# Block sums of feed-forward weights made in DRAM by accumulating transfers, and twelve more K pairs in seven products

## The chip, the cores and the metric

The kernel runs on one core of a Trainium2 chip. The metric is the device time of one execution in microseconds (us); lower is better. Weights and activations are float32. TensorE multiplies in the float32r format, and every float32 operand is split into a high and a low part (`hi`, `lo`), so a product of two operands is three matmuls: high x high, high x low, low x high.

## The reference

Two decoder layers on a sequence of 256 tokens with 2048 features. Layer 0 is a Mamba-2 SSD mixer, layer 1 differential attention; each is followed by a gated feed-forward of width 5632, with norms before and after.

```python
def swiglu(h, w_gate, w_up, w_down):
    return (jax.nn.silu(h @ w_gate) * (h @ w_up)) @ w_down

def reference(x, ...):
    for i in range(DEPTH):          # DEPTH = 2
        h = rmsnorm(x, norm_mix_pre[i])
        m = ssd_mixer(h, ...) if i % 2 == 0 else diff_attention(h, ...)
        x = x + rmsnorm(m, norm_mix_post[i])
        h = rmsnorm(x, norm_ffn_pre[i])
        x = x + rmsnorm(swiglu(h, ffn_w_gate[i], ffn_w_up[i], ffn_w_down[i]), norm_ffn_post[i])
    return x
```

## The kernel before

**Stages.** One TensorE stream runs through the SSD mixer (weights `w_zxbc`, then `w_so`), the first feed-forward (`w_g0`, `w_u0`, `w_d0`), attention, and the second feed-forward. The 256 tokens are two tiles `t` of 128. Weights come in blocks of 128 partitions x 4 x 512 floats (1 MB). A block is loaded by SP's queue into a `raw` buffer (three of them; in the feed-forwards two `rawm` buffers join, picked by a counter in `raw_tile`). `prep` makes `hi` by a copy on ScalarE and `lo` by a subtraction on VectorE.

**Pairs of column chunks.** In the feed-forwards `pair` works on two column chunks `c` and `c+1` of 512 columns at once. The contraction runs over K pairs: `kp` is a pair of 128-row K tiles. For one K pair the weights are a 2x2 grid of blocks (two K tiles by two chunks), and the activations another 2x2 grid (two token tiles by two K tiles). Multiplied out, a K pair takes eight products of three matmuls each. For the K pairs in the list `seven`, a Winograd form takes seven products: `p1`, `p5`, `p6`, `p7` and three sums that go straight into the accumulators. It needs sums and differences of the four weight blocks (`sh`, `sl`, split like a weight), and of the activations (`forms`, made by `make_form` into `ff` buffers, of which there are four in the pool's tag `xr`). The weight sums are made as follows: a GpSimd transfer adds block 1 onto block 0 of `raw` in SBUF while it loads (`accum_op=ALU.add`), and VectorE makes the other three in three additions, with four ScalarE copies and two more VectorE subtractions for `sh` and `sl`.

**Which K pairs.** `SEVEN = (2, 4, 6)` and `SEVEN_G = (2, 3, 4, 6)` name them for gate and up. `PARTS` walks the 11 chunks of the feed-forward in three parts, with the chunks of a part, then the K groups of the down projection that are ready behind it, then for chunk pairs 0 and 2 of the down projection the groups taken in seven products. `g_done` and `u_done` close a pair with the activation. The down projection's partial results of the first two parts are kept in the DRAM tiles `md`; those of the second part are added there by GpSimd's transfers (L733).

**The SSD stage.** Weights for z, B, C and x run through `mv` (24 matmuls a block). Beside them runs the scan: for every head group `g` and token tile `c`, `decay_load` fetches `mt` (SP), ScalarE makes the decay of it, and GpSimd multiplies it with `cbm` (L530). TensorE's `py` (L580) reads `mt`; its `pyo` (L612) reads `xdt`, which GpSimd has scaled (L608). GpSimd also takes the reciprocal roots `rs_g` (L97) of the gated norm, without which the transposes `pt_s` (L303) can't run.

**What sets the order.** The program is written with a step counter: `tick()` counts, and `later(k, fn)` puts `fn` k steps further. A list scheduler then places the instructions of each engine and queue, with the written order as priority; the place of an instruction can therefore differ from where the step counter puts it. At run time every engine and queue works through its own list in order, held by semaphores alone. A transfer started from GpSimd stands in GpSimd's list, and one from SyncE in SP's.

Of the kernel before, what the change touches and what calls it, by code (L numbers as in the profile page):

```python
# [16 lines left out]
P = 128  # L17
# [22 lines left out]
PARTS = [((10, 0, 1), (20, 0, 21, 1, 2, 3), {0: (21,), 2: (21, 2)}),  # L40
         ((2, 3, 4, 5), (4, 5, 8, 6, 9, 7, 10, 11), {0: (6, 7), 2: (6, 7)}),
# [4 lines left out]
def trunk_kernel(ctx, tc, x_rows, x_cols, vec_cols, vec64, post_rows, lam_rows,  # L46
# [177 lines left out]
    def pair(blocks, stat, seven, form, done):  # L224
# [20 lines left out]
        for kp, src in enumerate(blocks):  # L245
            raw = raw_tile()
            for c in range(2):
                nc.sync.dma_start(raw[:, 2 * c:2 * c + 2], src[c])
            if kp in seven:

                nc.gpsimd.dma_start(raw[:, 0:1], src[0][:, 1:2], accum_op=ALU.add)
# [12 lines left out]


            sh = hl[0].tile([P, 4, 512], F32R, tag="hi", name=f"sh{seq[0]}")
            sl = hl[0].tile([P, 4, 512], F32R, tag="lo", name=f"sl{seq[0]}")
            nc.vector.tensor_tensor(raw[:, 2], raw[:, 2], raw[:, 0], op=ALU.add)
            nc.scalar.copy(sh[:, 0], raw[:, 0])
            nc.scalar.copy(sh[:, 2], raw[:, 2])  # L270
            nc.vector.tensor_tensor(raw[:, 1], raw[:, 2], raw[:, 1], op=ALU.subtract)
            nc.scalar.copy(sh[:, 1], raw[:, 1])  # L272
            nc.vector.tensor_tensor(raw[:, 3], raw[:, 3], raw[:, 2], op=ALU.add)
            nc.scalar.copy(sh[:, 3], raw[:, 3])
            nc.vector.tensor_tensor(sl[:, 0:3], raw[:, 0:3], sh[:, 0:3].bitcast(F32), op=ALU.subtract)  # L275
            nc.vector.tensor_tensor(sl[:, 3], raw[:, 3], sh[:, 3].bitcast(F32), op=ALU.subtract)
# [5 lines left out]
            mm("p5", form(kp, 0), sh[:, 1], sl[:, 1], last)  # L282
            mm("p7", form(kp, 1), sh[:, 0], sl[:, 0], last)
# [488 lines left out]

    for half in range(2):
        if half == 0:
            later(2, dt_load)
            later(4, lambda: row_stats(0))
            later(5, lambda: (row_stats(1), dt_split()))
            later(7, halve)
            later(8, dt_product)
            later(8, lambda: later(1, make_rstd_bc(rstd_bc, rs0, lambda: s1.tile([P, P], F32, tag="dg", name="dg"))))  # L780
            later(10, dt_chain)
            later(15, dt_token)
            z_chunk(0, x_first_stat, z0_raw)
# [41 lines left out]
    def make_form(dct, key, stat, t512, keep=None):  # L825

        xf = t512("xf", (P, NT, 2, P))
        f = t512("f", (P, 4, P))
        for t in range(NT):
            for j in range(2):  # L830
                hi, lo = stat(key, j, t)
                nc.vector.tensor_tensor(xf[:, t, j], hi.bitcast(F32), lo.bitcast(F32), op=ALU.add)
        nc.vector.tensor_tensor(f[:, 0], xf[:, 1, 0], xf[:, 1, 1], op=ALU.subtract)
        nc.vector.tensor_tensor(f[:, 1], xf[:, 1, 0], xf[:, 0, 0], op=ALU.subtract)
        nc.vector.tensor_tensor(f[:, 2], xf[:, 0, 0], f[:, 0], op=ALU.subtract)
        nc.vector.tensor_tensor(f[:, 3], xf[:, 0, 1], f[:, 2], op=ALU.subtract)
        ff = dct[key] = xr_tile("ff", (P, 4, 2, P), F32R)
        split(ff[:, :, 0], ff[:, :, 1], f)
        if keep:
            nc.sync.dma_start(keep, ff.rearrange("p f h q -> p (f h q)").bitcast(F32))  # L840
# [22 lines left out]
    def ffn(wg, wu, wd, step, final):  # L863
# [17 lines left out]
        def kg_stat(kg, j, t):  # L881
            hi, lo = lookup(acts, (t, kg // 2))
            return hi[:, kg % 2 * 2 + j], lo[:, kg % 2 * 2 + j]

# [32 lines left out]
        for k, kp in enumerate(SEVEN_F):  # L917
            keep[kp] = dramp.tile([P, 8 * P], F32, name=f"form{step}_{kp}")
            later(1 + 3 * k, lambda kp=kp: make_form(forms, kp, kp_stat, t512, keep[kp]))
        mv([wu[10, k] for k in range(4)], u_stat, u_evac, LAG2)  # L920
        def form_later(k, kg):
            later(k, lambda: make_form(dforms, kg, kg_stat, t512))
# [5 lines left out]
        for pi, (part, kgs, two) in enumerate(PARTS):  # L928
# [12 lines left out]
            for c in part:  # L941
                if c < 10 and c % 2 == 0:
                    if c == part[-2]:
                        form_later(6, two[0][0])
                    pair(twos(wg, c), kp_stat, SEVEN_G if pi and c != part[-2] else SEVEN, form, g_done(c // 2))
                    if c == part[-2] and len(two[0]) > 1:
                        form_later(6, two[0][1])
                    pair(twos(wu, c), kp_stat, SEVEN_G if pi and c != part[-2] else SEVEN, form, u_done(c // 2))
            if pi == 0:
                form_later(8, two[2][1])  # L950
# [11 lines left out]
    ffn(w_g0, w_u0, w_d0, 1, False)  # L962
# [187 lines left out]
```

## Time and profile before

| | |
|---|---|
| time, median of 3 runs | 2525.58 us (2525.24 to 2525.67) |
| the profiled execution | 2525.76 us, span 2524.0 us |
| TensorE busy | 2505.5 us (99%), 11834 matmuls |
| VectorE, ScalarE, GpSimd busy | 1943.7 us (77%), 1412.9 us (56%), 233.4 us (9%) |
| SP's transfers (q1) | 503.96 MB, 57.5% of the 16 DMA engines' time |
| GpSimd's transfers (q0) | 35.13 MB, 7.0% |
| granted TensorE clock | 0.999 |

The SSD stage lies from 0 to some 700 us, the first feed-forward ends at 1357 us, the second starts near 1840 us. Matmuls overlap, so the mean length shown for one of them (about 390 ns) is more than what one adds to the time. A transfer's share is the time that its packets took, summed, over 16 engines times the stretch.

### The profile page before, as it was taken

To read this page: it belongs to the slowest core of one execution; us is meant where nothing else is said; L and a number is where in the kernel's file an instruction comes from. 1 tells how busy PE (TensorE), PEld (TensorE's weight loads), DVE (VectorE), ACT (ScalarE), POOL (GpSimd) and SP (SyncE) were. 2 spreads that over 40 slices of the span, in tenths; PEclk is the share of its full clock that TensorE was granted. 3 is DMA by queue.
4 is the path that set the end of the run, shared out by engine and by line. 5 is a ranking of instruction groups with operands and counts; after the bars stand their busy time and mean duration, and the time that the engine had idled before them with its cause. 6 is when DMAs were issued, how large, how long until landed. Compare 5 with 4: busy or idle time off the path is not lost.

```text
span 2524.0 us, 31572 instructions
## 1 busy us (share of the span) xinstructions
PE 2505.5 (99%) x11834; PEld 2066.3 (82%) x11834; DVE 1943.7 (77%) x2410; ACT 1412.9 (56%) x1915; POOL 233.4 (9%) x226
## 2 busy tenths in 40 slices
PE   9999999999999999999999999999999999999998
PEld 8878888888888888888888888887888888888886
DVE  6777547777688899978997765566688889878985
ACT  5767556666565455555554654455555465546553
POOL 0121000110110010001001100001100100010002
PEclk9999999999999999999999999999999999999999
DMA  7555556555786786768676544544776967686774
GB/s 286 194 169 183 193 189 200 169 182 186 254 275 204 251 256 212 253 216 259 214 253 229 192 149 167 184 150 148 249 228 205 295 217 231 220 271 220 229 246 153
DMA packets 143387, 541.44 MB, mean 215 GB/s; under 512 B 14401, under 2 KB 31105, under 8 KB 116225
## 3 DMA queue, kind: packets, MB, share of 16 engines
q1 hardware_dynamic: 125872, 503.96, 57.5%
q0 software_dynamic: 16992, 35.13, 7.0%
q8 instruction: 93, 1.52, 0.2%
q10 hardware_dynamic: 368, 0.32, 0.1%
q14 instruction: 62, 0.50, 0.1%
HBM read 520.41 MB, written 18.94 MB: 214 GB/s over the span
## 4 chain that ended last, share of the span: by engine, by line
PE 94%; DVE 2%; ACT 1%; issue 1%; DMA 1%; POOL 1%; SPq 0%; DVEq 0%; ACTq 0%; POOLq 0%
PE acc L242 38%; PE acc L191 34%; PE cp L242 9%; PE acc L216 5%; PE acc L218 2%; DVE lo L138 1%; PE sc L1026 1%; PE pt_f L303 1%; PE py L580 1%; DMA mt<-acum_d 1%; ACT hi L137 0%; PE ptx L666 0%; PE po L1062 0%; PE pc L487 0%; PE px L567 0%
## 5 line engine op out<-in xcount | busy, mean ns | idle before, releaser
L138 DVE TENSOR_TENSOR lo<-raw,hi 128x2048 fp32r<-128x2048 f32 (+2 forms) x401 | 733.9, 1833 | 302.1 <-ACT hi L137 298.0
L137 ACT CAST hi<-raw 128x2048 fp32r<-128x2048 f32 (+2 forms) x401 | 605.3, 1510 | 449.2 <-PE acc L191 140.3
L191 PE MATMUL acc<-hi,xT 128*128 128x512 f32 x1792 | 583.7, 397 | 0.1
L242 PE MATMUL acc<-hi,xT 128*128 128x512 f32 x1608 | 518.5, 390 | 0.0
L191 PEld LDWEIGHTS acc<-hi,xT 128*128 128x128 f32 x1792 | 335.7, 188 | 71.5 <-issue 3.0
L242 PEld LDWEIGHTS acc<-hi,xT 128*128 128x128 f32 x1608 | 301.8, 188 | 62.6
L191 PE MATMUL acc<-lo,xT 128*128 128x512 f32 x896 | 351.7, 393 | 1.4 <-DVE lo L138 1.4
L242 PE MATMUL acc<-lo,xT 128*128 128x512 f32 x804 | 312.9, 389 | 0.0
L138 DVE TENSOR_TENSOR lo<-rawm,hi 128x2048 fp32r<-128x2048 f32 (+1 forms) x87 | 181.8, 2089 | 35.3 <-ACT hi L137 32.1
L137 ACT CAST hi<-rawm 128x2048 fp32r<-128x2048 f32 (+1 forms) x87 | 152.7, 1756 | 96.6 <-PE acc L242 62.3
L191 PEld LDWEIGHTS acc<-lo,xT 128*128 128x128 f32 x896 | 168.6, 188 | 36.6 <-DVE lo L138 3.8
L216 PE MATMUL acc<-xT,hi 128*128 128x512 f32 x512 | 180.5, 398 | 0.0
L242 PEld LDWEIGHTS acc<-lo,xT 128*128 128x128 f32 x804 | 150.9, 188 | 31.4
L242 PE MATMUL acc<-hi,ah_f 128*128 128x512 f32 x450 | 176.1, 391 | 0.0
L242 PE MATMUL acc<-hi,al_f 128*128 128x512 f32 x450 | 175.2, 389 | 0.0
L242 PE MATMUL acc<-lo,ah_f 128*128 128x512 f32 x450 | 175.2, 389 | 0.0
L242 PE MATMUL cp<-sh,ff 128*128 128x512 f32 x516 | 172.8, 389 | 0.0
L218 PE MATMUL acc<-xT,lo 128*128 128x256 f32 x512 | 143.0, 281 | 0.0
L142 DVE SCALAR_TENSOR_TENSOR lo<-raw,cols,hi 128x512 fp32r<-128x512 f32 x128 | 92.4, 766 | 57.5 <-ACT hi L141 57.2
L141 ACT ACTIVATE hi<-raw,cols 128x512 fp32r<-128x512 f32 x128 | 84.6, 715 | 59.0 <-PE acc L191 41.3
L216 PEld LDWEIGHTS acc<-xT,hi 128*128 128x128 f32 x512 | 96.2, 188 | 23.0
L275 DVE TENSOR_TENSOR sl<-raw,sh 128x1536 fp32r<-128x1536 f32 x54 | 94.9, 1757 | 24.0 <-ACT sh L272 21.5
(298 smaller groups left out, 4101.4 us busy)
## 6 DMA issues: line engine op xcount, KB each, us to landing
raw<-in_w_zxbc_dram SPq DMA_DIRECT2D x77, 1024.0 KB, 4.8
raw<-in_w_d_dram SPq DMA_DIRECT2D x98, 512.0 KB, 5.8
raw<-in_w_g_dram SPq DMA_DIRECT2D x96, 512.0 KB, 6.0
raw<-in_w_u_dram SPq DMA_DIRECT2D x96, 512.0 KB, 5.9
raw<-in_w_qkv_dram SPq DMA_DIRECT2D x48, 1024.0 KB, 4.7
raw<-in_w_so_dram SPq DMA_DIRECT2D x32, 1024.0 KB, 4.7
rawm<-in_w_g_dram SPq DMA_DIRECT2D x64, 512.0 KB, 6.2
rawm<-in_w_u_dram SPq DMA_DIRECT2D x64, 512.0 KB, 5.7
```

The source lines that it names most:

```text
L137: nc.scalar.copy(hi, raw)
L138: nc.vector.tensor_tensor(lo, raw, hi.bitcast(F32), op=ALU.subtract)
L141: nc.scalar.activation(hi[:, j], raw[:, j], AF.Copy, scale=scale[j])
L142: nc.vector.scalar_tensor_tensor(lo[:, j], raw[:, j], scale[j], hi[:, j].bitcast(F32), op0=ALU.mult, op1=ALU.subtract)
L191: nc.tensor.matmul(acc[t], a, b[:, j], start=(i == 0 and j == 0 and q == 0), stop=(i == last and j == 1 and q == 2))
L216: nc.tensor.matmul(acc[ct], hi[:, j, cs], x.rearrange("p a s -> p (a s)"), start=(i == 0 and j == 0), stop=False)
L218: nc.tensor.matmul(acc[ct][:, :S], lo[:, j, cs], x[:, 0], start=False, stop=(i == last and j == 1))
L242: nc.tensor.matmul(acc[k], a, b, start=first and q == 0, stop=last and q == 2)
L275: nc.vector.tensor_tensor(sl[:, 0:3], raw[:, 0:3], sh[:, 0:3].bitcast(F32), op=ALU.subtract)
L303: nc.tensor.transpose(pt[:, j], src[:, j * P:(j + 1) * P], ident)
L580: nc.tensor.matmul(py[e * 64:(e + 1) * 64, a], xd[c][:, 2 * a + e], mts[c][:, 2 * a + e], start=True, stop=True)
L1026: nc.tensor.matmul(sc[c][:, h], qT[cp, h % 2, ts], kT[cp, h % 2, :nk * P], start=True, stop=True)
```

## The change

A new function `sums_of` is called ten times ahead of the SSD stage, for gate and up of chunk pairs 0, 2, 4, 6 and 8 of the first feed-forward. Each call makes a DRAM tile `bs` that holds, for K pairs 2 and 3, the four block sums that the seven products need. It copies three pieces from the weights (SP, DRAM to DRAM) and adds four pieces onto them (GpSimd, `accum_op`), two from the weights and two from the tile itself. `pair` gets a dictionary `ready`; for a K pair in it, it loads three blocks of the weights and the 1 MB of sums, and prepares both with `prep`, in place of the adding transfer and the VectorE additions. The first feed-forward now takes four K pairs in seven products in all its gate and up chunks; the down projections of both feed-forwards take three more. The forms 0 and 1 exchange places, and `make_form` makes them in fewer, wider instructions.

```diff
-PARTS = [((10, 0, 1), (20, 0, 21, 1, 2, 3), {0: (21,), 2: (21, 2)}),
-         ((2, 3, 4, 5), (4, 5, 8, 6, 9, 7, 10, 11), {0: (6, 7), 2: (6, 7)}),
+PARTS = [((10, 0, 1), (20, 0, 21, 1, 2, 3), {0: (21, 2), 2: (0, 21, 2)}),
+         ((2, 3, 4, 5), (4, 5, 8, 6, 9, 7, 10, 11), {0: (6, 7), 2: (5, 6, 7)}),
...
-    def pair(blocks, stat, seven, form, done):
+    def pair(blocks, stat, seven, form, done, ready={}):
...
+            if kp in ready:
+                nc.sync.dma_start(raw[:, 1:2], src[0][:, 1:2])
+                nc.sync.dma_start(raw[:, 2:4], src[1])
+                sums = raw_tile()
+                nc.sync.dma_start(sums, ready[kp])
+            else:
+                for c in range(2):
+                    nc.sync.dma_start(raw[:, 2 * c:2 * c + 2], src[c])
+                if kp in seven:
+                    nc.gpsimd.dma_start(raw[:, 0:1], src[0][:, 1:2], accum_op=ALU.add)
...
+            if kp in ready:
+                sh, sl = prep(sums)
+            else:
+                sh = hl[0].tile([P, 4, 512], F32R, tag="hi", name=f"sh{seq[0]}")
...
-            mm("p5", form(kp, 0), sh[:, 1], sl[:, 1], last)
-            mm("p7", form(kp, 1), sh[:, 0], sl[:, 0], last)
+            mm("p5", form(kp, 1), sh[:, 1], sl[:, 1], last)
+            mm("p7", form(kp, 0), sh[:, 0], sl[:, 0], last)
...
+    def sums_of(w, c, at):
+        d = dramp.tile([P, 2, 4, 512], F32, name=f"bs{len(ready0)}")
+        a, b = (w[c + e, 1].rearrange("p (k j) n -> p k j n", j=2) for e in range(2))
+
+        def begin():
+            for e in range(2):
+                nc.sync.dma_start(d[:, :, e], a[:, :, 0])
+            nc.sync.dma_start(d[:, :, 2:4], b)
+
+        def add(dst, src):
+            nc.gpsimd.dma_start(d[:, :, dst], src, accum_op=ALU.add)
+
+        later(at, begin)
+        later(at + 4, lambda: (add(0, a[:, :, 1]), add(1, b[:, :, 0])))
+        later(at + 9, lambda: add(2, d[:, :, 0]))
+        later(at + 13, lambda: add(3, d[:, :, 2]))
+        return {2: d[:, 0], 3: d[:, 1]}
+
+    ready0 = {}
+    for i, c in enumerate((0, 2, 4, 6, 8)):
+        for k, w in enumerate((w_g0, w_u0)):
+            ready0[(k, c)] = sums_of(w, c, 24 + 20 * (2 * i + k))
...
-        xf = t512("xf", (P, NT, 2, P))
+        xf = t512("xf", (P, 2, NT, P))
...
+        sums(key, xf)
+        b = xf.rearrange("p j t q -> p (j t) q")
+        nc.vector.tensor_tensor(f[:, 0:2], xf[:, 0, 1:2].to_broadcast([P, 2, P]), b[:, 0:4:3], op=ALU.subtract)
+        nc.vector.tensor_tensor(f[:, 2], xf[:, 0, 0], f[:, 1], op=ALU.subtract)
+        nc.vector.tensor_tensor(f[:, 3], xf[:, 1, 0], f[:, 2], op=ALU.subtract)
...
+                    four = bool(ready) or (pi > 0 and c != part[-2])
+                    pair(twos(wg, c), kp_stat, SEVEN_G if four else SEVEN, form, g_done(c // 2), ready.get((0, c), {}))
...
-    ffn(w_g0, w_u0, w_d0, 1, False)
+    ffn(w_g0, w_u0, w_d0, 1, False, ready0)
```

The steps at which the down projection's forms are made (`form_later`) move with the longer lists.

The order of the queues changes most in the first third of the SSD stage. First SP, from the third weight chunk on: `raw` is a weight load into SBUF, `acum_d` and `mt` belong to the scan, and `bs_167`, `bs_168` are the first two of the ten DRAM tiles (`bs_167` to `bs_176`). Before:

```order
L397 DMA rows<-in_x_rows_dram 128x2048 x2
L127 DMA raw<-in_w_zxbc_dram 128x2048 x8
L456 DMA acum_d<-tb 64x256
L127 DMA raw<-in_w_zxbc_dram 128x2048
L515 DMA mt<-acum_d 128x8x128 x2
L127 DMA raw<-in_w_zxbc_dram 128x2048 x9
```

And with the change:

```order
L127 DMA raw<-in_w_zxbc_dram 128x2048 x5
L786 DMA bs_167<-in_w_g_dram 256x512 x2
L127 DMA raw<-in_w_zxbc_dram 128x2048 x2
L787 DMA bs_167<-in_w_g_dram 256x1024
L127 DMA raw<-in_w_zxbc_dram 128x2048
L463 DMA acum_d<-tb 64x256
L786 DMA bs_168<-in_w_u_dram 256x512
L127 DMA raw<-in_w_zxbc_dram 128x2048
L522 DMA mt<-acum_d 128x8x128
L127 DMA raw<-in_w_zxbc_dram 128x2048
L522 DMA mt<-acum_d 128x8x128
L786 DMA bs_168<-in_w_u_dram 256x512
```

The copies start behind the fifth load, and go on in this way: the last of `bs_176` stands ahead of the thirtieth load.

Second, GpSimd at the first two head groups, with the multiplies `mt` and the scaled `xdt`. Before:

```order
L319 TENSOR_SCALAR dg<-ident,rs_in_281 128x128
L530 TENSOR_TENSOR mt<-mt,cbm 128x1024 x3
L608 TENSOR_TENSOR xdt<-xdt,ex_tok 128x512
L530 TENSOR_TENSOR mt<-mt,cbm 128x1024
L97 TENSOR_TENSOR rs_g_0_1265<-ms_g_0_1263,mhalf 128x1
```

With the change (ahead of these rows stand ten more adds, of `bs_167`, `bs_168` and `bs_169`, behind `dg`):

```order
L790 DMA bs_169<-bs_169 256x512 x2
L790 DMA bs_170<-in_w_u_dram 256x512
L537 TENSOR_TENSOR mt<-mt,cbm 128x1024
L790 DMA bs_170<-in_w_u_dram 256x512
L537 TENSOR_TENSOR mt<-mt,cbm 128x1024
L790 DMA bs_170<-bs_170 256x512 x2
L790 DMA bs_171<-in_w_g_dram 256x512 x2
L537 TENSOR_TENSOR mt<-mt,cbm 128x1024
L615 TENSOR_TENSOR xdt<-xdt,ex_tok 128x512
```

Thirteen adds now stand ahead of the first `mt`, and eighteen ahead of the first `xdt`.

Third, GpSimd at head groups 2 and 3, where the last adds are. Before:

```order
L97 TENSOR_TENSOR rs_g_0_1568<-ms_g_0_1566,mhalf 128x1
L97 TENSOR_TENSOR rs_g_1_1632<-ms_g_1_1630,mhalf 128x1
L530 TENSOR_TENSOR mt<-mt,cbm 128x1024 x3
L608 TENSOR_TENSOR xdt<-xdt,ex_tok 128x512
L530 TENSOR_TENSOR mt<-mt,cbm 128x1024
```

With the change:

```order
L97 TENSOR_TENSOR rs_g_1_1654<-ms_g_1_1652,mhalf 128x1
L790 DMA bs_175<-in_w_g_dram 256x512 x2
L537 TENSOR_TENSOR mt<-mt,cbm 128x1024
L790 DMA bs_175<-bs_175 256x512
L537 TENSOR_TENSOR mt<-mt,cbm 128x1024
L790 DMA bs_175<-bs_175 256x512
L790 DMA bs_176<-in_w_u_dram 256x512 x2
L790 DMA bs_176<-bs_176 256x512 x2
L537 TENSOR_TENSOR mt<-mt,cbm 128x1024
L615 TENSOR_TENSOR xdt<-xdt,ex_tok 128x512
```

All forty adds stand ahead of the third `mt` of this stretch and of its first `xdt`.

More of the change, by code (lines that the diff above doesn't have):

```diff
@@ L246, in pair @@
             raw = raw_tile()
[L247 to L251, printed above, removed]
+            if kp in ready:
[8 more added lines that the diff above has]
+                    nc.gpsimd.dma_start(raw[:, 0:1], src[0][:, 1:2], accum_op=ALU.add)
             if kp not in seven:
@@ L263, in pair @@
             hi, lo = prep(raw[:, 1:4])
[L266 to L276, printed above, removed]
+            if kp in ready:
+                sh, sl = prep(sums)
+            else:
+                sh = hl[0].tile([P, 4, 512], F32R, tag="hi", name=f"sh{seq[0]}")
+                sl = hl[0].tile([P, 4, 512], F32R, tag="lo", name=f"sl{seq[0]}")
+                nc.vector.tensor_tensor(raw[:, 2], raw[:, 2], raw[:, 0], op=ALU.add)
+                nc.scalar.copy(sh[:, 0], raw[:, 0])
+                nc.scalar.copy(sh[:, 2], raw[:, 2])
+                nc.vector.tensor_tensor(raw[:, 1], raw[:, 2], raw[:, 1], op=ALU.subtract)
+                nc.scalar.copy(sh[:, 1], raw[:, 1])
+                nc.vector.tensor_tensor(raw[:, 3], raw[:, 3], raw[:, 2], op=ALU.add)
+                nc.scalar.copy(sh[:, 3], raw[:, 3])
+                nc.vector.tensor_tensor(sl[:, 0:3], raw[:, 0:3], sh[:, 0:3].bitcast(F32), op=ALU.subtract)
+                nc.vector.tensor_tensor(sl[:, 3], raw[:, 3], sh[:, 3].bitcast(F32), op=ALU.subtract)
             mm("p1", stat(kp, 0, 0), hi[:, 1], lo[:, 1], last)
@@ L823, in xr_tile, with make_form @@
         return postp.tile(list(shape), dtype, tag="xr", name=name, bufs=4)
-    def make_form(dct, key, stat, t512, keep=None):
-        xf = t512("xf", (P, NT, 2, P))
+    def make_form(dct, key, sums, t512, keep=None):
+        xf = t512("xf", (P, 2, NT, P))
         f = t512("f", (P, 4, P))
[L829 to L836, printed above, removed]
+        sums(key, xf)
[3 more added lines that the diff above has]
+        nc.vector.tensor_tensor(f[:, 3], xf[:, 1, 0], f[:, 2], op=ALU.subtract)
         ff = dct[key] = xr_tile("ff", (P, 4, 2, P), F32R)
@@ L861, in trunk_kernel, with ffn @@
     xr_d = [[dramp.tile([P, 1024], F32, name=f"xr_d{t}{h}") for h in range(2)] for t in range(NT)]
-    def ffn(wg, wu, wd, step, final):
+    def ffn(wg, wu, wd, step, final, ready={}):
         acts, gt, forms, keep, dforms = {}, {}, {}, {}, {}
@@ L883, in kg_stat, with kp_sums, kg_sums @@
             return hi[:, kg % 2 * 2 + j], lo[:, kg % 2 * 2 + j]
+        def kp_sums(kp, xf):
+            x = xT[kp // 2][:, kp % 2 * 2:kp % 2 * 2 + 2].bitcast(F32)
+            nc.vector.tensor_tensor(xf.rearrange("p j t q -> p j (t q)"), x[:, :, 0], x[:, :, 1], op=ALU.add)
+        def kg_sums(kg, xf):
+            for t in range(NT):
+                hi, lo = (a[:, kg % 2 * 2:kg % 2 * 2 + 2].bitcast(F32) for a in lookup(acts, (t, kg // 2)))
+                nc.vector.tensor_tensor(xf[:, :, t], hi, lo, op=ALU.add)
         def form(kp, f):
@@ L918, in ffn @@
             keep[kp] = dramp.tile([P, 8 * P], F32, name=f"form{step}_{kp}")
-            later(1 + 3 * k, lambda kp=kp: make_form(forms, kp, kp_stat, t512, keep[kp]))
+            later(1 + 3 * k, lambda kp=kp: make_form(forms, kp, kp_sums, t512, keep[kp]))
         mv([wu[10, k] for k in range(4)], u_stat, u_evac, LAG2)
         def form_later(k, kg):
-            later(k, lambda: make_form(dforms, kg, kg_stat, t512))
+            later(k, lambda: make_form(dforms, kg, kg_sums, t512))
         md = [dramp.tile([P, D], F32, name=f"md{step}_{t}") for t in range(NT)]
@@ L942, in ffn @@
                 if c < 10 and c % 2 == 0:
+                    four = bool(ready) or (pi > 0 and c != part[-2])
+                    if c == part[-2] and not four:
+                        form_later(6, two[0][0])
+                    pair(twos(wg, c), kp_stat, SEVEN_G if four else SEVEN, form, g_done(c // 2), ready.get((0, c), {}))
                     if c == part[-2]:
[L944 to L948, printed above, removed]
+                        if four:
+                            form_later(9, two[0][0])
+                        if pi:
+                            form_later(12 if four else 6, two[0][1])
+                    pair(twos(wu, c), kp_stat, SEVEN_G if four else SEVEN, form, u_done(c // 2), ready.get((1, c), {}))
             if pi == 0:
-                form_later(8, two[2][1])
+                form_later(6, 2)
+                form_later(10, 0)
+            elif pi == 1:
+                form_later(9, 5)
             if pi < len(PARTS) - 1:
```

## The prediction

> **What bounds the kernel now.** I read the page first: busy shares, then the chain that ended last.
>
> ```profile
> PE 2505.5 (99%) x11834; PEld 2066.3 (82%) x11834; DVE 1943.7 (77%) x2410; ACT 1412.9 (56%) x1915; POOL 233.4 (9%) x226
> PE 94%; DVE 2%; ACT 1%; issue 1%; DMA 1%; POOL 1%; SPq 0%; DVEq 0%; ACTq 0%; POOLq 0%
> ```
>
> TensorE is busy 99% of the span and carries 94% of the chain. A product that goes is worth its time, and a wait put in front of TensorE costs its whole length, because nothing later has slack to give it back. The price of a product is read from the chain in order of time, and the cover around the change from the busy time by stretch. The columns of the stretches are length, then busy us (and instructions) of TensorE, its weight loads, VectorE, ScalarE and GpSimd, then TensorE's clock, the DMA engines' busy share and GB/s.
>
> ```profile
> 1013.19 17.00 PE acc L242 x75
> ...
> 40.00:60.00 20.00, 19.86 (x87) 15.46 (x86) 17.34 (x34) 8.69 (x10) 0.00 (x0) 1.00 0.58 190
> 60.00:80.00 20.00, 20.00 (x93) 16.39 (x92) 15.10 (x24) 17.46 (x34) 0.00 (x0) 1.00 0.72 234
> 80.00:100.00 20.00, 20.00 (x95) 16.43 (x94) 14.73 (x24) 11.79 (x17) 0.54 (x1) 1.00 0.49 165
> 100.00:120.00 20.00, 20.00 (x97) 16.49 (x96) 16.88 (x23) 12.12 (x22) 5.11 (x2) 1.00 0.71 230
> 120.00:140.00 20.00, 18.31 (x112) 14.66 (x111) 15.03 (x25) 14.02 (x27) 7.38 (x4) 1.00 0.37 132
> 140.00:160.00 20.00, 18.95 (x115) 15.12 (x114) 16.57 (x34) 16.43 (x35) 2.99 (x2) 1.00 0.64 211
> 160.00:180.00 20.00, 20.00 (x96) 16.26 (x95) 12.96 (x18) 12.06 (x18) 1.10 (x2) 1.00 0.44 152
> 180.00:200.00 20.00, 20.00 (x97) 16.54 (x96) 14.35 (x19) 10.68 (x15) 5.66 (x2) 1.00 0.56 186
> 200.00:220.00 20.00, 20.00 (x123) 16.29 (x122) 15.90 (x26) 15.66 (x32) 5.80 (x3) 1.00 0.53 171
> ...
> 836.00:1357.00 521.00, 521.00 (x2334) 431.84 (x2333) 457.06 (x469) 286.58 (x301) 42.87 (x53) 1.00 0.75 240
> ```
>
> A product costs 17.00/75 = 0.227 us. The first feed-forward (last row) has no idle TensorE at all. In the early SSD stage TensorE is nearly full too, and the DMA engines are busy between 0.37 and 0.72. That free part is what the new transfers must fit into.
>
> **What the change takes away.** Twelve K pairs go from eight products of three matmuls to seven: six in the first feed-forward (gate and up of chunks 0, 4 and 8, which had three sevens and now have four) and three in the down projection of each feed-forward. That is 12 x 3 = 36 matmuls, 36 x 0.227 = 8.2 us, all on the path. The terms p5 and p7 only exchange their forms: nothing.
>
> **What it adds in memory.** Each of ten `sums_of` calls copies 128x2x4x512 floats = 2.10 MB from weights to DRAM in three SP transfers, then adds four pieces of 0.52 MB in accumulating POOL transfers. Together that is 20.97 MB of copies and 40 adds, 20.97 MB again. The trace of before has neither form from memory to memory. The nearest rows are the program's first loads, at full rate, for the copies, and the accumulating loads of the feed-forward (SBUF target) and `md` adds (DRAM target) for the adds:
>
> ```profile
> DMA packets 1524, 3.82 MB, mean 382 GB/s; under 512 B 241, under 2 KB 346, under 8 KB 1524
> q1 hardware_dynamic: 1323, 3.66, 92.1%
> q10 hardware_dynamic: 201, 0.16, 9.4%
> ...
> q0 software_dynamic: 144, 0.26, 15.5%
> rawm<-in_w_u_dram POOLq DMA_DIRECT2D x1, 256.0 KB, 4.7
> ...
> q0 software_dynamic: 720, 1.31, 45.1%
> ...
> q0 software_dynamic: 1135, 2.28, 52.6%
> q1 hardware_dynamic: 1040, 3.79, 50.8%
> ```
>
> The first three rows are 3 to 13 us: with all 16 engines at 92.1 + 9.4 = 101.5% they moved 382 GB/s. So the copies take at least 20.97/0.382 = 55 us of all engines. The next two are 771 to 780.5 us: one 256 KB add took 15.5% of 9.5 us = 1.47 us. The row after is 1104 to 1120 us, five adds, four of them into DRAM: 45.1% of 16 us = 7.22, or 1.44 each. A DRAM target is no dearer. An add of 512 KB is thus put at 2.9 us, half the rate of a load. The last two rows are 1143 to 1165 us, where both queues had work all the time: the shares add up to 103%. I take from it that an engine serves one packet at a time, so POOL's transfers and SP's share one budget.
>
> **Where it lies, and what waits.** The delays given to the ten calls spread them over the stage, but in the built order all ten stand before the weights of the middle projection. The queues' order, shown above with the change, puts the copies between the fifth and the thirtieth `raw` load of SP, and 18 adds before the first `xdt` on POOL and all 40 before the third `xdt`. GpSimd works in order: a `mt` multiply or `xdt` behind an add waits until that add's own semaphores have come. TensorE's order here is as before to within two rows, so it stops at the `py` or `pyo` that needs them. SP's later loads, too, stand behind the copies.
>
> ```profile
> 19.19 32.18 SPq L127 DMA_DIRECT2D raw<-in_w_zxbc_dram  x8
> 64.33 46.41 SPq L127 DMA_DIRECT2D raw<-in_w_zxbc_dram  x9
> ...
> 125.88 1.07 POOL L608 TENSOR_TENSOR xdt<-xdt,ex_tok 128x512 f32<-128x512 f32 x1
> 207.32 2.40 POOL L530 TENSOR_TENSOR mt<-mt,cbm 128x1024 f32<-128x1024 f32 x1 [17.38 <-DVE cbm L529]
> 209.66 1.06 POOL L608 TENSOR_TENSOR xdt<-xdt,ex_tok 128x512 f32<-128x512 f32 x1
> ...
> 134.39 1.02 PE L612 MATMUL pyo<-xdt,cbx 128*128 128x512 f32 x2
> ...
> 218.17 1.02 PE L612 MATMUL pyo<-xdt,cbx 128*128 128x512 f32 x2
> ```
>
> The third `pyo` runs at 218.17 and needs the `mt` (2.40) and `xdt` (1.06) that now stand behind add 40, which must have issued by 214.7; 39 adds have landed by then. Copies start near the fifth load, about 40 us. The DMA work wanted is 55 + 39 x 2.9 = 168 us. Free between 40 and 214.7 us are 20 x (0.42+0.28+0.51+0.29+0.63+0.36+0.56+0.44) + 14.7 x 0.47 = 76.7 us. The shortfall, 168 - 77 = 91 us, is what TensorE stands still. It shows early: the first `pyo`, at 134.39, stands behind 18 adds (17 landed, 49 us) and about 4.5 sums of copies (25 us), 74 us of work against 39 us free.
>
> Ends of this term. Low: the loads already there were slower than full rate; their 32.5 MB (GB/s times length of the rows) at 382 GB/s take 85 us of the 174.7, which frees 90; then 55 + 112 - 90 = 77. High: a copy of 2 KB rows costs as much as an add of them, 40 x 2.9 = 116 instead of 55; then 152. I take 91, since the copies are plain transfers and nearest to the load row. On GpSimd the 40 issues are bounded by 0 and 40 x 0.87 us (row below, a 128-row issue), but they run while the chain waits for landings: nothing more.
>
> The Trainium skill, "DMA: Bandwidth & Descriptors", section "Latency and other measured facts", gives HBM-to-HBM copies 207 to 214 GB/s per direction at best. By that the copies take 98 us instead of 55 and the stall is 134; no row of this trace shows such a copy.
>
> **In the feed-forwards.** A `ready` pair loads 1 MB of sums and 0.25 MB less of `raw`: 20 x 0.79 MB/0.382 = 41 us more DMA; it drops 14 adds (34 to 20) at 1.47 = 21 us, and the three new sevens below add 4. A share of 0.75 over 521 us becomes about 0.79, hidden by the five-buffer prefetch. Sums use ten tiles in a pair of chunks where eight were; the bound is 0 to one landing. VectorE does less for the 14 ready pairs that were sevens (three adds fewer each) and more for the twelve new sevens (one more subtraction of a tile, and three adds in the six of the down projections); with 457 busy of 521 us this hides behind TensorE at 100%, and with that cover gone one K pair's chain would show. `make_form` has fewer and longer instructions, three more forms for each feed-forward, and an `ff` buffer taken over while its old form is still read: ScalarE could then wait with `hi` casts queued behind. The bound is 0 to about 4 us (cast and subtraction of one tile, 1756 and 2089 ns below); TensorE's idle there is 0 now, so I take 0.
>
> ```profile
> L251 POOL DMA_DIRECT2D raw<-in_w_g_dram x20: 852/867/905, 738.3 to 2347.6; - x20
> DMA to landing us min/median/max: 3.9/7.1/11.4
> ...
> DMA to landing us min/median/max: 7.8/10.0/12.5
> ...
> L138 DVE TENSOR_TENSOR lo<-rawm,hi 128x2048 fp32r<-128x2048 f32 (+1 forms) x87 | 181.8, 2089 | 35.3 <-ACT hi L137 32.1
> L137 ACT CAST hi<-rawm 128x2048 fp32r<-128x2048 f32 (+1 forms) x87 | 152.7, 1756 | 96.6 <-PE acc L242 62.3
> ```
>
> **Sum.** The profiled execution took 2525.8 us (span 2524.0, 1.8 around it); the median of the runs is 2525.6. 2525.8 - 8.2 + 91 = 2608.6, say 2609.
>
> **Rivals.** Slower by the chain alone: if the engines overlapped the two queues, the adds would still follow one another. In a sum the third add waits for the first and the fourth for the third, two landings for each sum. From about 47 us, at the 8 to 10 us of the landing rows (7.1 median of single loads, 10.0 for four `md` adds), ten sums end between 207 and 247, a stall of 0 to 32: 2518 to 2550. For it: the landings are measured. Against it: the 103% row.
>
> Faster, all hidden: 2525.8 - 8.2 = 2517.6. Mechanism: an add's packet time is mostly waiting on memory in which the engine can serve others, and landings stay short, so only copies count. It decides where an add takes under (77 - 55)/39 = 0.56 us of the engines, a fifth of the row. It would also come out if the calls did spread over the stage as their delays say: from 40 to 640 us the engines are free 44%, 260 us, more than 168. The built order excludes that.
>
> Dearer copies: writing to DRAM beside reading it halves the rate, a copy then costs what an add does: 2525.8 - 8.2 + 152 = 2670. For it: adds, too, touch memory twice and are half as fast. Against it: adds into DRAM cost no more than into SBUF. The Trainium skill's figure above would end this case at 2652.
>
> **Chances.** Engines the bound, 2595 to 2625 around 2609: 0.58. Chain alone: 0.14. Hidden: 0.12. Dearer copies: 0.12. Something else: 0.04. The range goes from the top of the chain's case, 2550, to the dear copies', 2670, and leaves out the hidden case and most of the chain's. About 0.2% is what a measurement here can tell from no change: faster 0.12, same 0.03, slower 0.85. Cases above 2530 hold most of it; the likeliest one's own range is 2595 to 2625.
>
> **What would show it.** Right: DMA near 0.9 or more from 50 to 300 us; the 40 adds on POOL with landings of 8 us or more, the last one issued near 300; TensorE waiting on GpSimd at `py`, `pyo` or the gated transposes from about 130 us, for some 90 us in all; after the SSD stage the same pace, 8 us shorter over the rest. Wrong: a DMA share under 0.8 there, adds' packet time far from 2.9 us, or TensorE idle in the feed-forward.

## The result and the profile after

The changed kernel takes 2636.98 us (median of 4 runs, 2634.32 to 2642.49); the kernel before took 2525.47 us beside it. The ratio is 1.0445, 95% interval 1.0433 to 1.0457: slower by 111.5 us, where 83 were predicted. The profiled execution took 2634.32 us, span 2632.5. The page of the changed kernel, first its busy shares and the engines' shares of the chain that ended last, then TensorE's granted clock and the DMA engines' share in 40 slices of 66 us:

```profile
PE 2521.1 (96%) x11798; PEld 2069.7 (79%) x11798; DVE 1953.5 (74%) x2346; ACT 1429.9 (54%) x1907; POOL 259.1 (10%) x258
...
PEclk9968799999999999999999999999999999999999
DMA  9999855555477778778867654444486786697764
...
PE 83%; DMA 7%; DVE 4%; issue 4%; ACT 1%; POOL 1%; SPq 0%; DVEq 0%; ACTq 0%; POOLq 0%
```

36 matmuls are gone, and TensorE's share of the chain fell from 94% to 83%. The DMA share is 0.9 or more in the first four slices, which are 263 us. Where the time went is read from the same pieces of the chain in both kernels (start in us, length, work). Before:

```profile
620.77 70.78 PE acc L191 x312
...
747.84 9.33 PE acc L242 x41
...
1357.35 38.09 PE acc L191 x168
...
1861.61 9.12 PE acc L242 x40
...
2470.91 21.08 PE acc L191 x94
```

After:

```profile
731.46 70.78 PE acc L191 x312
...
858.57 9.35 PE acc L242 x41
...
1466.44 38.09 PE acc L191 x168
...
1969.38 9.12 PE acc L242 x40
...
2578.40 21.09 PE acc L191 x94
```

The delay is 110.7 us at the end of the SSD stage and at the start of the first feed-forward, 109.1 at its end, 107.8 at the start of the second feed-forward and 107.5 at its end. So the whole loss is made in the SSD stage, and the two feed-forwards win 1.6 and 0.3 us. Another 1.3 us is won in the attention between them and 1.0 lost again at the end (the spans differ by 108.5); neither was followed. The stretches of that stage (columns as in the prediction):

```profile
60.00:80.00 20.00, 17.48 (x73) 13.60 (x72) 11.91 (x20) 11.62 (x23) 2.64 (x3) 0.91 1.05 328
...
160.00:180.00 20.00, 8.44 (x39) 6.18 (x37) 9.95 (x11) 3.88 (x6) 6.54 (x5) 0.79 1.06 248
...
300.00:320.00 20.00, 5.90 (x43) 5.02 (x44) 3.55 (x9) 7.23 (x21) 3.03 (x3) 0.54 0.81 172
320.00:340.00 20.00, 19.85 (x95) 15.91 (x94) 18.64 (x25) 12.15 (x20) 4.53 (x3) 1.00 0.84 234
```

From 160 to 180 us TensorE works 8 of 20 us while the DMA engines are full, and it is back at 19.85 as soon as GpSimd has given out its last addition. GpSimd's timeline there (start, length, instruction, and in brackets what it waited for):

```profile
317.85 0.87 POOL L790 DMA_DIRECT2D bs<-bs  x1 [9.45 <-DMA bs<-bs]
318.42 2.71 POOL L537 TENSOR_TENSOR mt<-mt,cbm 128x1024 f32<-128x1024 f32 x1
320.78 1.34 POOL L615 TENSOR_TENSOR xdt<-xdt,ex_tok 128x512 f32<-128x512 f32 x1
```

This is the `mt` and the third `xdt` of the prediction: 207.32 before, 318.42 after, 111.1 us later. Who waited, from the waits of TensorE up to 900 us, and of ScalarE from 40 to 330 us (waiter, releaser, us in total, times, longest):

```profile
PE px L574 <- DVE xg L482: 38.6, 6, 18.4
PE pc L494 <- ACT tk L500: 28.4, 3, 22.8
PE acc L191 <- ACT hi L137: 17.3, 3, 14.9
...
PE pyo L619 <- POOL xdt L615: 0.7, 1, 0.7
...
ACT y L640 <- POOL rs_g L97: 58.6, 4, 22.0
ACT mt L530 <- DMA mt<-acum_d: 37.1, 5, 18.7
```

TensorE hardly waits on GpSimd itself. ScalarE does: it stands in its order at the gate's scaling (L640), which needs `rs_g` from GpSimd, and at the scan's decay (L530), which needs the late `mt` load. What TensorE needs is queued behind: the evacuations `tk`, the casts `hi`, and the `th` from which VectorE makes `xg`. The loads from 40 to 320 us (KB each, median us from issue to landing), and over the whole program the landing of `mt` (min, median, max), after and then before:

```profile
raw<-in_w_zxbc_dram SPq DMA_DIRECT2D x26, 1024.0 KB, 12.8
mt<-acum_d SPq DMA_DIRECT2D x8, 512.0 KB, 16.5
...
DMA to landing us min/median/max: 6.2/8.1/29.3
...
DMA to landing us min/median/max: 6.3/7.0/9.1
```

### The profile page after: what moved, and what is told of

Read it like the earlier page. It is cut to its first block, busy times and chain, and to the rows that moved or that the text cites. A ratio compares the mean times of both kernels' runs of the same rounds, so it can differ in the third digit from the quotient of the medians.

```text
span 2632.5 us, 31546 instructions
## 1 busy us (share of the span) xinstructions
PE 2521.1 (96%) x11798; PEld 2069.7 (79%) x11798; DVE 1953.5 (74%) x2346; ACT 1429.9 (54%) x1907; POOL 259.1 (10%) x258
## 4 chain that ended last, share of the span: by engine, by line
PE 83%; DMA 7%; DVE 4%; issue 4%; ACT 1%; POOL 1%; SPq 0%; DVEq 0%; ACTq 0%; POOLq 0%
PE acc L242 33%; PE acc L191 29%; PE cp L242 9%; PE acc L216 5%; DMA mt<-acum_d 3%; PE acc L218 2%; DVE lo L138 2%; DMA raw<-in_w_zxbc_dram 1%; DMA bs<-bs 1%; PE sc L1069 1%; DMA bs<-in_w_g_dram 1%; PE pt_f L310 1%; ACT hi L137 1%; DMA raw<-in_w_g_dram 1%; PE py L587 1%
## 5 line engine op out<-in xcount | busy, mean ns | idle before, releaser
L138 DVE TENSOR_TENSOR lo<-raw,hi 128x2048 fp32r<-128x2048 f32 (+2 forms) x413 | 758.3, 1840 | 343.1 <-ACT hi L137 334.2
L137 ACT CAST hi<-raw 128x2048 fp32r<-128x2048 f32 (+2 forms) x413 | 625.8, 1516 | 467.5 <-PE acc L191 140.7
L191 PE MATMUL acc<-hi,xT 128*128 128x512 f32 x1792 | 593.4, 403 | 17.3 <-ACT hi L137 17.3
L242 PE MATMUL acc<-hi,xT 128*128 128x512 f32 x1564 | 508.9, 390 | 0.0
L191 PEld LDWEIGHTS acc<-hi,xT 128*128 128x128 f32 x1792 | 341.8, 191 | 91.3 <-ACT hi L137 18.3
L191 PE MATMUL acc<-lo,xT 128*128 128x512 f32 x896 | 357.6, 399 | 3.4 <-DVE lo L138 3.3
L242 PEld LDWEIGHTS acc<-hi,xT 128*128 128x128 f32 x1564 | 293.6, 188 | 61.1 <-DVE sx L732 0.4
L242 PE MATMUL acc<-lo,xT 128*128 128x512 f32 x782 | 305.1, 390 | 0.3 <-DVE lo L138 0.3
L137 ACT CAST hi<-rawm 128x2048 fp32r<-128x2048 f32 (+1 forms) x95 | 165.0, 1737 | 136.5 <-PE acc L242 109.3
L138 DVE TENSOR_TENSOR lo<-rawm,hi 128x2048 fp32r<-128x2048 f32 (+1 forms) x95 | 196.4, 2067 | 45.3 <-ACT hi L137 41.1
L191 PEld LDWEIGHTS acc<-lo,xT 128*128 128x128 f32 x896 | 171.8, 192 | 41.7 <-DVE lo L138 8.0
L242 PEld LDWEIGHTS acc<-lo,xT 128*128 128x128 f32 x782 | 146.8, 188 | 32.5 <-DVE lo L138 2.6
L242 PE MATMUL acc<-hi,ah_f 128*128 128x512 f32 x408 | 159.6, 392 | 0.0
L242 PE MATMUL acc<-lo,ah_f 128*128 128x512 f32 x408 | 158.9, 390 | 0.2 <-DVE lo L138 0.2
L242 PE MATMUL acc<-hi,al_f 128*128 128x512 f32 x408 | 158.9, 389 | 0.0
L242 PE MATMUL cp<-sh,ff 128*128 128x512 f32 x468 | 157.8, 390 | 0.0
L282 DVE TENSOR_TENSOR sl<-raw,sh 128x1536 fp32r<-128x1536 f32 x49 | 86.1, 1758 | 35.9 <-ACT sh L279 34.3
```

The source lines that it names most:

```text
L137: nc.scalar.copy(hi, raw)
L138: nc.vector.tensor_tensor(lo, raw, hi.bitcast(F32), op=ALU.subtract)
L191: nc.tensor.matmul(acc[t], a, b[:, j], start=(i == 0 and j == 0 and q == 0), stop=(i == last and j == 1 and q == 2))
L242: nc.tensor.matmul(acc[k], a, b, start=first and q == 0, stop=last and q == 2)
```

## The experiments

Two theories stood against each other after the result. Engine budget: the added transfers take more DMA engine time than is free before the third `xdt`, and the shortfall is the stall. Chain: each addition waits for the one before it, so GpSimd is late whatever the engines have free. A third question was where the gain of the 36 matmuls went. Times of the kernel before beside the runs were 2525.30 to 2525.77 us.

**Additions out, copies kept.** The 40 additions are not made.

```diff
-        later(at + 4, lambda: (add(0, a[:, :, 1]), add(1, b[:, :, 0])))
-        later(at + 9, lambda: add(2, d[:, :, 0]))
-        later(at + 13, lambda: add(3, d[:, :, 2]))
```

> The copies stay, the 40 adds are left out (the sums are then only copies of blocks). DMA engines as the budget: 55 us of copies against 77 us free before 215 us, so 0 to 15 us of stall, 2520 to 2540. Copies as dear as adds (116 us): 39 us of stall, about 2560. Chain of adds: no chain, no stall, about 2522.

2525.51 us, one run. The SSD stage's long piece, at 620.77 us before, starts at 621.29: no stall is left, so the copies by themselves are hidden.

**No chain.** The third and fourth addition of a sum take a piece of the weights in place of a piece of the tile, so they wait for no landing of an addition before them.

```diff
-        later(at + 9, lambda: add(2, d[:, :, 0]))
-        later(at + 13, lambda: add(3, d[:, :, 2]))
+        later(at + 9, lambda: add(2, a[:, :, 1]))
+        later(at + 13, lambda: add(3, b[:, :, 0]))
```

> The third and fourth add of a sum take their source from the weights and no longer from the tile itself, so no add waits for another's landing; bytes, packets and places in the queues are the same (the sums' values are different ones). DMA engines as the budget: stall stays at 85 to 115 us, 2610 to 2640. Chain of landings on GpSimd: two landings of some 12 us for each sum go, the stall falls to 0 to 30, 2520 to 2555.

2631.64 us, one run: 5 us less than the changed kernel. GpSimd still waited 181 us at its additions, now for copies to land, so this run alone does not clear a chain through all landings. But that one addition of a sum waits for another is not what costs. The next run leaves the chain whole and changes only what a transfer costs.

**Plain copies in place of additions.**

```diff
-            nc.gpsimd.dma_start(d[:, :, dst], src, accum_op=ALU.add)
+            nc.gpsimd.dma_start(d[:, :, dst], src)
```

> The 39 accumulating transfers on GpSimd's queue become plain copies of the same pieces between the same places, with the same order and the same waits; the sums therefore hold copies instead of sums. Theory of the engine budget: an accumulating transfer took 130 / 40 = 3.26 us of the sixteen engines' time in the stretch from 40 to 320 us, a plain copy of 0.524 MB costs some 55 x 0.524 / 20.97 = 1.4 us, so the added work falls from some 180 us to 55 + 57 = 112 us against the 77 us free before: a stall of some 35 us is left, 2555 us (2535 to 2575). Rival, the GpSimd engine's waits for each transfer to land (the number of transfers decides, not their kind): as long a stall as in the changed kernel, 2600 us or more.

2580.48 us, one run: 54.9 us over the kernel before, just above the budget's upper end of 2575, and 20 us under the least of the chain's. With the same chain half the stall is gone, so a chain whose landings take as long whatever the engines do falls here. The landings became shorter too (9.9 us instead of 13.2 in the median), so this run alone does not clear a chain of landings that lengthen. Against that one stands the share of the DMA engines in the changed kernel: 0.97 or more in each 20 us from 40 to 260 us, and 0.81 to 1.07 from there to 320. They were not idle for want of GpSimd. What a transfer costs can now be read for each kind. The rows are from 40 to 320 us (queue, packets, MB, share of 16 engines): SP's queue before, SP's queue with the copies alone, SP's and GpSimd's queues in the changed kernel, then GpSimd's with plain copies.

```profile
q1 hardware_dynamic: 16832, 51.58, 55.1%
...
q1 hardware_dynamic: 24674, 71.93, 76.3%
...
q1 hardware_dynamic: 20181, 52.25, 55.1%
q0 software_dynamic: 10644, 20.52, 46.6%
...
q0 software_dynamic: 5760, 20.97, 24.9%
```

SP's copies: (76.3% - 55.1%) x 280 = 59.4 us for 20.35 MB, 61.2 us for the 20.97 MB. The additions: 46.6% x 280 = 130.5 us for 20.52 MB, some 39 of the 40, or 3.35 us each (the expectation had divided by 40). A plain copy on GpSimd's queue: 24.9% x 280 / 40 = 1.74 us. These times are not stretched by waiting in full engines: SP's queue moved 52.25 MB in 55.1% in the changed kernel and 51.58 MB in 55.1% before, and in the spread kernel below, from 40 to 640 us, 32 additions (16.78 MB) took 18.2% of 600 us, 3.41 us each, with both queues together at 76.6%. With the 76.7 us that the prediction counted as free, the budget gives for the changed kernel 61.2 + 130.5 - 76.7 = 115 us, measured 111.1; with plain copies 61.2 + 39 x 1.74 - 76.7 = 52, and the third `xdt` stands at 266.18 us there, 56.5 later than before; with copies alone a negative number, measured no stall. The budget comes out to some 4 us in both stalled kernels. The 130.5 and the 1.74 are read from these same runs, so this shows that the terms add up, not that they could have been known.

**Larger pieces in the scan's load.** `acum_d` is laid out so that a partition's piece of an `mt` load is one run of 4096 bytes, not eight of 512. Once on the changed kernel, and once on the spread kernel below.

```diff
-    acum_d = dramp.tile([NH, S], F32, name="acum_d")
+    acum_d = dramp.tile([2, NH, P], F32, name="acum_d")
...
-        nc.sync.dma_start(mt, acum_d[g * 8:g * 8 + 8, c * P:(c + 1) * P].partition_broadcast(P))
+        nc.sync.dma_start(mt.rearrange("p h q -> p (h q)"), acum_d[c, g * 8:g * 8 + 8].rearrange("h q -> (h q)").partition_broadcast(P))
```

> The changed kernel with the same other layout of acum_d (mt loads in pieces of 4096 bytes) and nothing else. Theory of the engine budget: the 111 us come from transfer work that has to be done before GpSimd passes its 40th addition, so the layout takes at most the few us that the loads themselves cost: 2620 us or more, GpSimd's last addition at 310 us or later. Rival, that the stall is made by the late mt loads in ScalarE's order (37 us waited there, and what hangs on them): 2600 us or less.

2627.98 us, one run: 9 us less, and the stall stays: GpSimd's last addition goes out at 318.19 us, 317.85 in the changed kernel. The late `mt` loads are how the stall reaches ScalarE, not what makes it.

**Spread.** Each copy and addition is pinned behind the last instruction written before it on its engine, so it stays where the step counter puts it.

```diff
+    def behind(engine):
+        last = next(i for i in reversed(nc.cur_bb.bb.instructions) if i.engine == engine.engine)
+        return tc.issue_after(last)
...
+            with behind(nc.gpsimd):
+                nc.gpsimd.dma_start(d[:, :, dst], src, accum_op=ALU.add)
```

> Each copy and add is held behind the instruction of its queue that was written just before it, so the ten sums keep the places of their step numbers, over 45 to 640 us. DMA engines as the budget: 168 us of work against some 260 us free, 0 to 10 us of stall; with the 2 to 8 us gained in the feed-forwards 2517 to 2530. Chain of landings: 26 us lie between the steps of a sum, more than two landings, so little waiting too; 2517 to 2530. If GpSimd still holds up rs_g or xdt by a landing each time, 10 to 40 us more.

2574.21 us (2573.45 to 2575.99), ratio 1.0193, interval 1.0178 to 1.0208. More than half the loss is gone, and 48.4 us are left that this expectation did not have. Two stretches of this kernel, and two pieces of its chain:

```profile
200.00:220.00 20.00, 16.82 (x82) 13.54 (x80) 12.65 (x21) 9.65 (x16) 0.54 (x1) 1.00 1.01 285
340.00:360.00 20.00, 20.00 (x90) 16.57 (x89) 9.98 (x15) 11.27 (x18) 2.64 (x3) 1.00 1.04 322
...
204.21 14.93 DMA mt<-acum_d
239.47 11.53 DMA mt<-acum_d
```

In the middle projection, at 340 us, the engines are full and TensorE loses nothing. In the scan, at 200 us, they are as full, and TensorE loses 3.2 of 20 us, behind an `mt` load that landed after more than 14 us instead of 7.0 (median before). A second such load, at 239.47 us, took more than 11. So there is a cost that the budget up to the third `xdt` does not hold, and it hangs on the scan. The larger pieces on top of the spread:

> The spread kernel (every copy and addition held at its place in its engine's order), with acum_d laid out so that each partition's piece of a mt load is one run of 4096 bytes instead of eight runs of 512 bytes; the values are the same. In the spread kernel ScalarE waited 39.4 us for late mt<-acum_d loads (median landing 12.9 us against 7.0 before) and TensorE 32.3 us for xg behind it. Theory that these loads are hurt by their small pieces beside the additions: landing falls to 8 us or less, the waits nearly go, and of the 48 us lost to the kernel before at least 30 come back: 2522 to 2545 us. Rival, that the loads are late because SyncE's queue gives them out late (it stood 6 to 10 us between the two loads of a pair) or because the engines have no time left: 2565 us or more, with ScalarE's wait for mt about as long.

2568.96 us (2565.4 to 2569.45), ratio 1.0174, interval 1.0158 to 1.0189: 5 us back of 48, so small pieces are not the reason; the loads' median landing was 12.4 us, 12.9 in the spread kernel.

**Fewer sums, between the scans or in the scan.** Only K pair 3 of chunks 0, 4 and 8 is summed in memory, 6 sums in 24 additions of half the size, pinned. The same 36 matmuls are gone. Two kernels differ only in the step at which they begin, 80 or 26:

```diff
...
-        a, b = (w[c + e, 1].rearrange("p (k j) n -> p k j n", j=2) for e in range(2))
+        a, b = (w[c + e, 1, :, 2:4] for e in range(2))
...
-        return {2: d[:, 0], 3: d[:, 1]}
+        return {3: d}
...
-    for i, c in enumerate((0, 2, 4, 6, 8)):
+    for i, c in enumerate((0, 4, 8)):
...
-            ready0[(k, c)] = sums_of(w, c, 24 + 20 * (2 * i + k))
+            ready0[(k, c)] = sums_of(w, c, 80 + 9 * (2 * i + k))
```

> Sums in memory only where the kernel before has no seven: K pair 3 of chunks 0, 4 and 8 of the gate and of the up projection, 6 sums in 24 additions of 262 KB in place of 20 in 40 of 524 KB; the same 36 matmuls are gone. Each copy and addition is held at its place in its engine's order, and all of them fall between the two scans, in the output projection from some 250 to 400 us, where no mt load is under way. Engine time, from the rows of the changed kernel: copies 6 x 1.05 MB at 382 GB/s = 16 us, additions 24 x 1.6 us = 39 us, 55 us in all, against some 150 us x 0.45 = 67 us free there. Theory that the spread kernel lost its time where additions and the small-piece loads of the scan ran together: TensorE stays busy 20.00 of 20 us in those stretches, no wait over 1 us is left in the scans, and the time is that of the down projections alone (2523.7 us) less some 2 us gained in the first feed-forward: 2520 to 2524 us. Rival, that any addition during the SSD stage costs TensorE its time (the spread kernel lost 48 us for 40 additions): 24 half-size additions cost some 15 us, 2535 us or more.

> The same 6 sums, pinned in the same way, but begun 54 steps earlier, so that copies and additions fall among the chunk projections and the loads of the first scan (40 to 260 us). Theory of the collision with the scan's loads: ScalarE waits for late mt<-acum_d loads, TensorE for xg behind it, some 5 us at each of 3 to 5 places: 2533 to 2548 us. Rival, that only the amount of transfer work decides (55 us against 77 us free from 40 to 214.7 us): no stall, 2520 to 2526 us.

Between the scans: 2524.24 us (2523.58 to 2525.10), ratio 0.9995, interval 0.9986 to 1.0004. In the scan: 2539.35 us (2538.39 to 2542.51), ratio 1.0057, interval 1.0044 to 1.0070. Between the scans, a stretch, a wait of TensorE and the landings of the `mt` loads (min, median, max):

```profile
340.00:360.00 20.00, 20.00 (x90) 16.57 (x89) 9.33 (x11) 10.37 (x14) 3.23 (x6) 1.00 1.04 296
...
PE px L574 <- DVE xg L482: 1.8, 4, 0.8
...
DMA to landing us min/median/max: 6.0/6.9/8.0
```

In the scan, the same, with SP's and GpSimd's timelines ahead of the worst load and that load in the chain:

```profile
220.00:240.00 20.00, 16.99 (x80) 13.47 (x79) 12.55 (x18) 7.10 (x11) 3.46 (x4) 1.00 0.95 214
...
PE px L574 <- DVE xg L482: 16.7, 5, 11.1
...
ACT mt L530 <- DMA mt<-acum_d: 18.1, 4, 12.3
...
DMA to landing us min/median/max: 6.0/7.3/18.2
...
221.50 1.96 POOL L796 DMA_DIRECT2D bs<-in_w_g_dram  x2
...
222.49 1.32 SPq L791 DMA_DIRECT2D bs<-in_w_u_dram  x2
...
226.99 18.07 DMA mt<-acum_d
```

The same work costs nothing in one place and 15 us in the other. Two additions and three copies went out in the 5.5 us ahead of the load at 226.99, and it took 18 us instead of 7. ScalarE stood 12.3 us at it, and TensorE 11.1 us at `px` behind that. The amount of transfer work in the stage does not decide here. But the engines were full just while the load was under way: their share is 0.98 from 227 to 245 us, and it is 1.00 and 1.04 over the two late loads of the spread kernel (204.21 to 219.14 and 239.47 to 251.00 us). That agrees with the same budget over the length of one landing, but does not show it. With the copies alone the engines stood at 0.91 to 0.98 from 60 to 200 us and no `mt` load took more than 9.4 us, so a share just short of full, with no additions in it, was not enough.

**More lead for the scan's loads.** `mt` is given out up to three steps earlier, in the kernel with the sums in the scan and in the spread kernel.

```diff
-        later(4, lambda: mts.update({c: decay_load(g, c) for c in range(2)}))
+        later(1, lambda: mts.update({c: decay_load(g, c) for c in range(2)}))
```

> The 6 sums amid the first scan as in the run before, with one change: the two mt loads of a group are given out up to three steps earlier (SyncE now passes them one to three weight loads sooner), while ScalarE uses them where it did. Theory that the scan has no lead for these loads (they landed 6 to 9 us after their issue in the kernel before, just in time, and 18 us with additions and copies ahead of them): the earlier issue covers the longer landing, ScalarE's 18.1 us of waits for mt and TensorE's 16.7 us for xg shrink to under 5 us, 2523 to 2530 us, though the landing stays long. Rival, that the additions slow the scan in another way (the loads' slots come free late, or the engines are full): 2536 us or more.

> The spread kernel with all 20 K pairs and its 40 additions held in place (2574.2 us), and the mt loads up to three steps earlier in the same way. By the lead theory most of its 48 us goes: 2525 to 2545 us, as far as free slots let the loads go out earlier. By the rival 2565 us or more.

With 6 sums 2540.65 us (2539.74 to 2541.17): nothing gained, the lead theory missed. With 20 K pairs 2547.77 us (2545.98 to 2548.56), ratio 1.0088, interval 1.0073 to 1.0103: 26.4 us better than the spread kernel, just outside the range given. In the first of the two TensorE's waits at `px` fell from 16.7 to 10.0 us, but it lost 3.6 us more from 80 to 100 us and 2.3 more from 140 to 160, and the worst load did not move, as the chain shows:

```profile
228.03 15.59 DMA mt<-acum_d
```

It went out at 228.03 us against 226.99 without the edit, so the edit gave it no lead. That is why the miss does not decide against the theory, and the 26 us of the other kernel speak for it, but do not settle it. Whether these loads wait behind the additions in the engines' queues or only share the engines with them was not separated either; the piece size alone is excluded.

**The gain of the matmuls.** First the added sevens by the old way, without sums in memory (VectorE makes the sums); then the down projections' sevens alone.

```diff
...
-                    four = bool(ready) or (pi > 0 and c != part[-2])
+                    four = step == 1 or (pi > 0 and c != part[-2])
```

> No block sums in DRAM; the twelve more K pairs take the old way (adding transfer into SBUF, VectorE additions). Both theories of the stall: no stall in the SSD stage, so 2525.5 - 8.2 = 2517.3 us if the products' gain is whole. The changed kernel's trace gave back only 1.6 us in the first feed-forward and 0.3 in the second where 6.1 and 2.0 were summed up; if VectorE or the down projection's forms eat the gain, and not the block sums, this one ends near 2522 to 2524 too. If the ready pairs ate it, 2517 to 2519.

```diff
...
-                    four = bool(ready) or (pi > 0 and c != part[-2])
+                    four = pi > 0 and c != part[-2]
```

> The changed kernel without any sums in memory and with the first feed-forward's gate and up projections as in the kernel before; only the three further K pairs in seven products of each down projection are left (18 matmuls of 0.2267 us fewer, 4.1 us of TensorE time). If each matmul taken out is gained, as the prediction had it: 2521.4 us, ratio 0.9984. If the sevens that go by the old route cost back what they save because their operands come late (in the changed kernel the second feed-forward gained 0.3 us of 2.0): 2524.5 to 2525.5 us, ratio 0.9996 to 1.

By the old way 2529.04 us (2528.77 to 2533.49), ratio 1.0016, interval 1.0007 to 1.0026: slower than before with 36 matmuls fewer. The down projections alone: 2523.70 us (2523.43 to 2524.62), ratio 0.9994, interval 0.9985 to 1.0003: some 1.9 us of the 4.1, and not told apart from no change. The six sevens of gate and up, then, by the old way cost 2529.04 - 2523.70 = 5.3 us, though they save 6 x 3 x 0.227 = 4.1. VectorE is one reason. All waits of TensorE in the first feed-forward by the old way end on it, and the kernel before has none there. Then VectorE's busy time, third in these rows: before and with the down projections alone at 828 us, and the old way over the stretch whose row of before is in the prediction.

```profile
PE cp L242 <- DVE sl L282: 1.7, 4, 0.8
PE acc L242 <- DVE lo L138: 1.6, 7, 0.2
...
828.00:868.00 40.00, 40.00 (x186) 33.21 (x185) 37.50 (x46) 18.60 (x20) 2.85 (x4) 1.00 0.74 260
...
828.00:868.00 40.00, 40.00 (x187) 33.28 (x186) 39.44 (x52) 20.97 (x26) 3.17 (x4) 1.00 0.75 238
...
836.00:1357.00 521.00, 517.20 (x2286) 420.86 (x2285) 477.20 (x493) 294.61 (x328) 47.96 (x58) 1.00 0.76 239
```

VectorE is at 39.44 of 40 us where it was at 37.50, and 477.20 of 521 where it was at 457.06. In the chain of the down projections' kernel, pieces of it stand from 909 to 916 us, where the chain of before had TensorE alone; one of them:

```profile
914.05 1.77 DVE sl L282
```

That VectorE is the only reason is not shown. With the sums made in memory between the scans it is as busy over the same stretch (476.92 of 521 us), and the first feed-forward (from the L242 piece near 747 us to the attention's first L191 piece) takes 608.53 us there, against 613.96 by the old way and 608.90 with the down projections alone. So sums in memory take back 5.4 us against the old way, but of the 4.1 us that the six sevens should save only 0.4 are seen. The chain of the old way also passes through four loads of `w_d` from 1314 to 1343 us, 4.8 to 6.7 us each; what these cost was not separated.

## Why the prediction was right, and where its terms were off

**The mechanism and the size.** The predicted 2609 us is 28 us short of the measured time; the range 2550 to 2670 holds it. Right: one budget of the DMA engines for both queues, the place where it binds (the third `xdt`, 111.1 us later), the stall's start in the first third of the stage, and nothing given back later. The two terms of the sum missed in the same direction: 20 us in the stall, and 5.6 in the gain (8.2, of which 111.1 - 108.5 = 2.6 are seen in the span), so no error hid another.

**The stall, 91 us in the sum, 111 measured.** The copies were put at 55 us and took 61; the 39 additions were put at 2.9 us each and took 3.35, 130.5 us instead of 113. With the prediction's own 76.7 us of free time that gives 115. Thus the two durations taken from neighbouring rows were 10 and 13% low, and their sum stands against a fixed amount, so the stall came out 18% low. The bound of 152, copies as dear as additions, did not hold: a plain copy on GpSimd's own queue takes 1.74 us, an addition of the same bytes 3.35. The prediction gave a time by a figure of the Trainium skill, "DMA: Bandwidth & Descriptors", section "Latency and other measured facts" (207 to 214 GB/s, from which it estimated 98 us of copies); by engine time the copies ran at 20.35 MB / 59.4 us = 343 GB/s, and the trace does not agree with that reading of the page.

**How the stall reaches TensorE.** The prediction had TensorE stop at `py` and `pyo` behind GpSimd, from about 130 us. It lost 2.5 us already from 60 to 80 us, and waited at `pyo` 0.7 us in all. The path was ScalarE's order, at `rs_g` and the `mt` loads. The prediction named later `raw` loads, and they are on the chain, but it gave them no size; the `mt` loads' landing (16.5 us in the median from 40 to 320 us) was the step left out. Two pieces of the chain show both:

```profile
100.09 16.95 DMA raw<-in_w_zxbc_dram
...
121.83 29.33 DMA mt<-acum_d
```

**The gain, 8.2 us in the sum, some 2 measured in the feed-forwards.** This term was mis-sized by a factor of four. The prediction hid VectorE's extra work behind TensorE at 100%, and named what would show if that cover were gone. It was gone in parts: a mean of 457 of 521 us hides stretches of 40 us in which VectorE is above 0.93, and the sevens were added there. How much of the missing gain is VectorE's stays open, as said above. In the changed kernel late loads came on top, as its chain shows with two `raw` loads from 1007 us on:

```profile
1007.14 7.63 DMA raw<-in_w_g_dram
```

**The rivals.** Chain alone: fell when the additions no longer waited for one another, 2631.64 us where it would give 2518 to 2550. All hidden: would need additions under 0.56 us, they take 3.35; hidden by spreading was excluded by the built order and came true only where the additions kept clear of the scans. Dearer copies: fell.

## What to carry over

Before work is moved to memory-side transfers, add up the engine time of all queues against the free share up to the first instruction that has to stand behind them; here an accumulating transfer took 1.9 times a copy on the same queue. Then look at where in the program it runs, and at the engines' share while a load is under way, not only over the stage: the same 24 additions cost nothing beside a stage whose loads are prefetched, and 15 us beside loads that are given out just in time. And when matmuls are saved by more work on another engine, read that engine's busy time in the stretch of the saving, not in the mean over the stage.

## What was not expected of the hardware

TensorE's granted clock fell in the stretches where it stood still: 0.54 and 0.79 in two rows of the changed kernel above, and back at 1.00 in the first 20 us behind the last addition. What that adds to the time of the stall was not measured. An `mt` load of 512 KB, 6.3 to 9.1 us from issue to landing before, took up to 29.3 us beside additions, with SP's weight loads of twice the size at a median of 12.8 us instead of 4.8; with larger pieces it still took up to 26.1.
